# One expert input block beside each group of routing weights, one-hot tiles built a group ahead, and weights read back by eight expert blocks

## The chip, the cores and the metric

The kernel runs on one core of one Trainium2 chip. The metric is the device time of one execution in microseconds (us). Several executions are timed and their median is given. One more execution is recorded with the hardware profiler.

## What is computed

One layer of a backbone for 512 latent tokens (768 with the context) of width 1024: a mixer (state-space scan, pooling, neighbourhood attention), an output projection, and then a product-key expert network, the PEER part. The change touches the last part alone:

```python
def peer_ffn(u, w_q, sub_keys, u_tab, v_tab):
    q = (t @ w_q).reshape(n_tok, 8, 2, 128)
    s = einsum('thid,hikd->thik', q, sub_keys)
    v1, i1 = top_k(s[:, :, 0], 16); v2, i2 = top_k(s[:, :, 1], 16)
    ...
    idx = take_along_axis(cand_idx, pos)          # 128 experts of 16384 for each token
    g = softmax(top_s)
    act = gelu(einsum('tkd,td->tk', u_tab[idx], x))
    return einsum('tk,tkd->td', g * act, v_tab[idx])
```

So each of 512 tokens picks 8 x 16 = 128 experts out of 16384. An expert has an input row (in `peer_u`) and an output row (in `peer_v`), both of width 1024.

## The kernel before

The expert tables are cut into 128 blocks of 128 experts. For 384 of the 512 tokens (three tiles of 128) the kernel works densely: for every block `a` it multiplies the tokens with all 128 input rows (here an **input block** or U block: `u_block`, 24 matmuls of 384 columns, since every product is made of three float32r products of a high and a low part), applies gelu, multiplies with a 128 x 384 tile of routing weights that is zero wherever a token did not choose an expert, and multiplies the result with the 128 output rows (a **value block** or V block: `e_v`, 18 matmuls of 512 columns, summed in PSUM over all 128 blocks). The last 128 tokens are worked by gathering: for each of 128 **slots** `k`, GpSimd (POOL) gathers one expert row (input and output row side by side) for each of the 128 tokens (`g_load`), VectorE (DVE) makes the dot product with the token (`g_dot`), ScalarE (ACT) its gelu and its weight (`g_act`), and DVE adds the weighted output row to a sum (`g_acc`). The rows sit in four buffers.

An input block needs nothing of the routing, so 74 of the 128 (`NAHEAD`, the list `AHEAD`) are made ahead of the expert loop: `ahead_steps` is a generator, and each `next(ahead)` makes one of them. In a step it first takes the low parts left from the step before (DVE), then fetches coming blocks, splits the block two steps on into its high part (ACT, line 177) and leaves the low part (DVE, line 180) to the next step, then runs the 24 matmuls, the gelu (ACT) and writes the result to DRAM (`act_d`, issued by ACT).

The **routing weights stage** (`weights_T`, lines 1559 to 1594) turns expert numbers and softmax weights into dense weight tiles. 384 tokens are taken in 48 groups of eight (three calls of 16). For each group DVE builds one-hot tiles from the numbers: `oi` (line 1567, 16 bit, 2048 elements for each partition) and `ow`, the one-hot times the weight's high and low part (line 1571, two instructions). TensorE (PE) multiplies them, 16 matmuls of 128 columns for each group (lines 1578 and 1579, into `gdps`), ACT copies the results into a staging tile (`stg`, line 1581, two for each group), and after each fourth group 2 MB are written to DRAM (`gd_d`). Beside it run input blocks (`next(ahead)` where `q8 in UQ`: three of four groups) and slots of the gathered tokens (one for four groups, so 12 here). All is issued under `manual_schedule`: each engine takes its instructions in the order in which the code is written.

The **expert loop** (lines 1759 to 1794) goes over all blocks. At step `i` SyncE (SP) issues reads for blocks ahead: the stored result of an input block made ahead (`acl`, at `i+6`) or the input rows (`wraw<-in_peer_ut`, at `i+6`), the output rows (`wraw<-in_peer_uv`, at `i+4`) and, for every fourth block, the routing weights of four blocks (`e_weights`, 768 KB in runs of 512 bytes, at `i+5`). DVE and ACT multiply by the weights and split for block `i+1`, PE runs the input block `i+2` if it was not made ahead (54 are left), and then value block `i`. The gathers' slots 12 to 127 are spread evenly over the first 121 steps (`kG`). SP takes its reads in order, and a read waits at the head of the queue until its buffer is free or its source is written.

Of the kernel before, what the change touches and what calls it, by code (L numbers as in the profile page):

```python
# [7 lines left out]
F32 = mybir.dt.float32  # L8
# [138 lines left out]
NAHEAD = 74  # L147
# [3 lines left out]
def build(tc, A, out, dbg=None):  # L151
# [1405 lines left out]
    gq = {}  # L1557

    def weights_T(t):
        for q8 in range(16):  # L1560
            if q8 % 4 == 0:
                stg = sg.tile([P, P, TQ], F32, name="stg")

            def tb(ap):
                return ap[:, t * 16 + q8].rearrange("p w (g c) -> p (w g) c", c=2).unsqueeze(2).broadcast_to([P, 8, P, 2])
            oi = gs2.tile([P, 2, 4, P, 2], F16, name="oi", bufs=3)
            V.tensor_tensor(oi.rearrange("p w g b c -> p (w g) b c"), iotaA.unsqueeze(1).broadcast_to([P, 8, P, 2]), tb(ixT), ALU.is_equal)
            ob, oa = oi[:, 0], oi[:, 1]
            ow = gs2.tile([P, 2, 4, P, 2], F16, name="ow", bufs=3)
            for w in range(2):  # L1570
                V.tensor_tensor(ow[:, w], oa, tb(gwT)[:, w * 4:w * 4 + 4], ALU.mult)
            oh, ol = ow[:, 0], ow[:, 1]
            for q4 in range(2):
                ps = psD.tile([P, 4, P], F32, name="gdps")
                for j in range(4):
                    tt = q4 * 4 + j
                    pr, c = tt // 2, tt % 2
                    PE.matmul(ps[:, j, :], ob[:, pr, :, c], oh[:, pr, :, c], start=True, stop=False)
                    PE.matmul(ps[:, j, :], ob[:, pr, :, c], ol[:, pr, :, c], start=False, stop=True)  # L1579
                t0 = q8 % 4 * 8 + q4 * 4  # L1580
                S.activation(stg[:, :, t0:t0 + 4].rearrange("p a t -> p t a"), ps, AF.Copy, scale=1.0 / GSCALE)  # L1581
            if q8 % 4 == 3:
                (nc.gpsimd if t == 2 and q8 == 15 else nc.scalar).dma_start(gd_d[t * 4 + q8 // 4], stg)
            if q8 in UQ:
                next(ahead, None)
            k = t * 4 + q8 // 4
            gq[0] = stg
            if q8 % 4 == 0:
                if k:
                    g_acc(k - 1)  # L1590
                    g_load(k + 3)
                g_dot(k)
            elif q8 % 4 == 1:
                g_act(k)

    UQ = (0, 1, 3, 4, 5, 7, 8, 9, 11, 12, 13, 15)
# [21 lines left out]
    go_ahead(2)  # L1618
# [8 lines left out]
    for t in range(3):  # L1627
        weights_T(t)
    g_acc(11)
    g_load(15)  # L1630
# [10 lines left out]
    gl = glp.sb("gl", bufs=3)  # L1641
# [24 lines left out]
    def e_weights(a):  # L1666

        if a % 4 == 0:
            n = NQ if a else NQ - 1
            gd = gds[a // 4] = gls[a // 4 % 2].tile([P, NQ, 4 * TQ], F32, name="gd", bufs=1)  # L1670
            nc.sync.dma_start(gd[:, 0:n, :], gd_d[0:n, :, a:a + 4, :].rearrange("q b a t -> b q (a t)"))
            if n < NQ:
                G.tensor_copy(gd[:, n, :], gq[0][:, 0:4, :].rearrange("p a t -> p (a t)"))

# [7 lines left out]
    def e_w(a):  # L1682

        x = ac.pop(a)
        xq = x.rearrange("p (q t) -> p q t", q=NQ)
        V.tensor_tensor(xq, xq, gds[a // 4][:, :, a % 4 * TQ:(a % 4 + 1) * TQ], ALU.mult)  # L1686
# [13 lines left out]
    def f_load():  # L1700

        nc.sync.dma_start(fgr, A["rowg"][:, D:2 * D])
        for t in (3, 0, 1, 2):
            nc.sync.dma_start(hx[:, t, :], h_d[t * P:(t + 1) * P, :])
        row_bc(g2r, psu, 2, 2)

    def f_mul(t, hf):

        if hf == 0:
            sqs[t] = gt.tile([P, 2 * D], F32, name="row")  # L1710
            fss[t] = e1.tile([P, 2], F32, name="fss", bufs=2)
        sq = sqs[t]
        hs = slice(hf * 512, (hf + 1) * 512)
        src = accT[t][hf] if t < 3 else accG[:, hs]
        if "peer" in dbg:
            V.tensor_copy(sq[:, hs], src)
            nc.sync.dma_start(dbg["peer"][t * P:(t + 1) * P, hs], sq[:, hs])
        V.tensor_tensor(sq[:, hs], src, g2r[:, hs], ALU.mult)
        (V if t == 2 else G).tensor_tensor(hx[:, t, hs], sq[:, hs], hx[:, t, hs], ALU.add)

    def f_sq(t, hf):
        hs = slice(hf * 512, (hf + 1) * 512)
        S.activation(sqs[t][:, hs], hx[:, t, hs], AF.Square, accum_out=fss[t][:, hf:hf + 1])
# [5 lines left out]
    def f_gain(t, hf):  # L1729
        hs = slice(hf * 512, (hf + 1) * 512)  # L1730
        (V if t == 2 else G).tensor_tensor(sqs[t][:, D + hf * 512:D + hf * 512 + 512], hx[:, t, hs], fgr[:, hs], ALU.mult)
# [18 lines left out]
    kG = [12 + min(P - 12, (i * (P - 12) + 120) // 121) for i in range(P + 1)]  # L1750
    with order:
# [6 lines left out]
        hx = e1.tile([P, NX, D], F32, name="hx")  # L1758
        for i in range(-6, P + 1):
            within(lambda a: e_load(a, 0), i + 6)  # L1760
            within(lambda a: e_load(a, 1), i + 4)
            if i > -5:
                within(e_weights, i + 5)
# [19 lines left out]
            if i == 64:  # L1783
                f_load()
            if i == P - 4:
# [58 lines left out]
```

## Time and profile before

| what | before |
| --- | --- |
| median of 3 runs | 1888.75 us |
| lowest and highest | 1887.59 and 1889.18 us |
| the profiled execution's own time | 1889.47 us |
| its span in the profile | 1887.6 us |
| PE busy, DVE busy, ACT busy, POOL busy | 96%, 72%, 45%, 18% |
| DMA, mean over the span | 237 GB/s |

The profile gives for every instruction its start and duration, and for idle time of an engine what ended it. A matmul's duration is modelled and overlaps the next one, so the spacing of starts, not the busy share, tells how fast PE goes. The routing weights stage lasts from about 887 to 1101 us, the expert loop from there to the end. A read or write through DMA is given by the time from its issue to its landing.

### The profile page before, as it was taken

What the parts mean: (1) busy time and instruction counts of PE and PEld (TensorE: products, weight loads), DVE (VectorE), ACT (ScalarE), POOL (GpSimd) and SP (SyncE); (2) the same over time, 40 slices, a digit from 0 to 9 for tenths busy, and PEclk for the clock granted to TensorE, in tenths of its full rate; (3) what the DMA queues carried; (4) which work ended last, traced back from release to release, by engine and by line L of the source; (5) the groups of instructions that cost most, each with busy time, mean ns of one, the idle gap of its engine ahead of it and who ended that gap; (6) DMA issues with size and microseconds to landing.
All of it is one profiled execution on the core that took longest, in us unless ns stands there. A gap on an engine that the chain in (4) does not pass through costs nothing.

```text
span 1887.6 us, 26321 instructions
## 1 busy us (share of the span) xinstructions
PE 1805.8 (96%) x9703; PEld 1521.7 (81%) x9703; DVE 1363.1 (72%) x2681; ACT 845.7 (45%) x1552; POOL 348.4 (18%) x261
## 2 busy tenths in 40 slices
PE   7999999986899999999999999999999999999997
PEld 4677776654677888999988898888888888888886
DVE  5553137797653459987788878887888887888875
ACT  4332226534653433345767654443443443443444
POOL 1101300151012544420011011111111111111103
PEclk9999999997999999999999999999999999999999
DMA  9546332217423533474787889999999999999971
GB/s 364 165 140 200 85 123 67 68 53 229 149 74 100 163 111 111 135 253 156 266 301 287 289 317 387 351 332 357 356 328 353 373 351 351 370 325 345 366 256 62
DMA packets 210193, 446.74 MB, mean 237 GB/s; under 512 B 13424, under 2 KB 137072, under 8 KB 192112
## 3 DMA queue, kind: packets, MB, share of 16 engines
q1 hardware_dynamic: 172192, 259.25, 41.1%
q0 software_dynamic: 18576, 136.32, 18.7%
q10 hardware_dynamic: 19296, 49.49, 7.2%
q8 instruction: 76, 1.25, 0.3%
q14 instruction: 53, 0.43, 0.1%
HBM read 394.81 MB, written 52.30 MB: 237 GB/s over the span
## 4 chain that ended last, share of the span: by engine, by line
PE 82%; DVE 7%; ACT 6%; issue 2%; DMA 1%; POOL 0%; ACTq 0%; DVEq 0%; SPq 0%; POOLq 0%
PE pv L188 9%; PE pv L187 9%; PE pv L189 9%; PE pu L187 8%; PE pu L189 8%; PE pu L188 8%; PE acc L187 5%; PE acc L189 5%; PE acc L188 5%; ACT stg L1581 2%; PE acc L419 2%; PE acc L421 2%; PE acc L423 1%; DVE wl L180 1%; ACT wh L177 1%
## 5 line engine op out<-in xcount | busy, mean ns | idle before, releaser
L180 DVE TENSOR_TENSOR wl<-wraw,wh 128x1024 fp32r<-128x1024 f32 x290 | 355.2, 1241 | 190.9 <-ACT wh L177 182.3
L177 ACT ACTIVATE wh<-wraw 128x1024 fp32r<-128x1024 f32 x324 | 336.1, 1053 | 223.8 <-PE acc L188 76.8
L187 PE MATMUL pu<-u2h,wh 128*128 128x384 f32 (+2 forms) x1040 | 354.8, 341 | 0.0
L189 PE MATMUL pu<-u2h,wl 128*128 128x384 f32 (+2 forms) x1040 | 350.4, 337 | 1.5 <-DVE wl L180 1.5
L188 PE MATMUL pu<-u2l,wh 128*128 128x384 f32 (+2 forms) x1040 | 350.3, 337 | 0.0
L188 PE MATMUL pv<-wl,wwh 128*128 128x512 f32 x768 | 303.2, 395 | 0.0
L187 PE MATMUL pv<-wh,wwh 128*128 128x512 f32 x768 | 303.1, 395 | 0.0
L189 PE MATMUL pv<-wh,wwl 128*128 128x512 f32 x768 | 303.1, 395 | 0.0
L1524 POOL DMA_INDIRECT row<-in_peer_uv,idxG x128 | 138.7, 1084 | 844.4 <-DVE accG L1538 746.0
L187 PEld LDWEIGHTS pu<-u2h,wh 128*128 128x128 f32 x1040 | 196.6, 189 | 3.1 <-ACT g2r L1092 0.7
L188 PEld LDWEIGHTS pu<-u2l,wh 128*128 128x128 f32 x1040 | 196.6, 189 | 2.3
L189 PEld LDWEIGHTS pu<-u2h,wl 128*128 128x128 f32 x1040 | 196.3, 189 | 1.9 <-DVE wl L180 1.8
L189 PEld LDWEIGHTS pv<-wh,wwl 128*128 128x128 f32 x768 | 144.4, 188 | 34.4
L188 PEld LDWEIGHTS pv<-wl,wwh 128*128 128x128 f32 x768 | 144.4, 188 | 32.1 <-DVE wl L180 0.2
L187 PEld LDWEIGHTS pv<-wh,wwh 128*128 128x128 f32 x768 | 144.3, 188 | 32.0
L1538 DVE SCALAR_TENSOR_TENSOR accG<-row,wG,accG 128x1024 f32<-128x1024 f32 x127 | 162.5, 1279 | 0.0
L1529 DVE CUSTOM_DVE_ANT_0 row<-row,u2G 128x1024 f32<-128x1024 f32 x128 | 156.2, 1220 | 0.0
L1686 DVE TENSOR_TENSOR act<-act,gd 128x384 f32<-128x384 f32 x54 | 31.3, 579 | 131.3 <-ACT act L1680 131.3
L177 ACT ACTIVATE wwh<-acl 128x384 fp32r<-128x384 f32 x74 | 38.9, 526 | 191.4 <-DVE acl L1686 157.8
L1680 ACT ACTIVATE act<-pu 128x384 f32<-128x384 f32 x54 | 26.6, 492 | 207.3 <-PE pu L189 207.3
L1581 ACT ACTIVATE stg<-gdps 128x512 f32<-128x512 f32 x96 | 98.0, 1161 | 26.7 <-PE gdps L1579 21.9
L180 POOL TENSOR_TENSOR wl<-wraw,wh 128x1024 fp32r<-128x1024 f32 x34 | 81.7, 2403 | 112.5 <-ACT wh L177 94.0
(403 smaller groups left out, 3111.7 us busy)
## 6 DMA issues: line engine op xcount, KB each, us to landing
wraw<-in_peer_ut SPq DMA_DIRECT2D x128, 512.0 KB, 5.4
wraw<-in_peer_uv SPq DMA_DIRECT2D x128, 512.0 KB, 9.5
gd<-gd_d SPq DMA_DIRECT2D x31, 768.0 KB, 12.7
gd_d<-stg ACTq DMA_DIRECT2D x11, 2048.0 KB, 6.7
wraw<-in_w_in SPq DMA_DIRECT2D x36, 512.0 KB, 4.1
acl<-act_d SPq DMA_DIRECT2D x74, 192.0 KB, 6.6
act_d<-act ACTq DMA_DIRECT2D x72, 192.0 KB, 5.0
kT<-in_ada_w SPq DMA_DIRECT2D x18, 512.0 KB, 4.8
```

The source lines that it names most:

```text
L177: S.activation(hi, full, AF.Copy)
L180: (eng or V).tensor_tensor(lo, full, hi.bitcast(F32), ALU.subtract)
L187: PE.matmul(ps, ah, bh, start=start, stop=False)
L188: PE.matmul(ps, ah, bl, start=False, stop=False)
L189: PE.matmul(ps, al, bh, start=False, stop=stop)
L419: PE.matmul(px, h[:, k, :], uh[:, k, :], start=s, stop=False)
L421: PE.matmul(px, h[:, k, :], ul[:, k, :], start=False, stop=False)
L1524: G.indirect_dma_start(out=rows[k], out_offset=None, in_=A["peer_uv"], in_offset=bass.IndirectOffsetOnAxis(ap=idxG[:, k:k + 1], axis=0))
L1529: V.tensor_tensor_reduce(row[:, 0:D], row[:, 0:D], u2G, 1.0, 0.0, ALU.mult, ALU.add, actG[:, k:k + 1])
L1538: V.scalar_tensor_tensor(accG, row[:, D:2 * D], wG[:, k:k + 1], accG, ALU.mult, ALU.add)
L1581: S.activation(stg[:, :, t0:t0 + 4].rearrange("p a t -> p t a"), ps, AF.Copy, scale=1.0 / GSCALE)
L1686: V.tensor_tensor(xq, xq, gds[a // 4][:, :, a % 4 * TQ:(a % 4 + 1) * TQ], ALU.mult)
```

## The change

- `NAHEAD` goes from 74 to 86, so 12 more input blocks are made ahead and 42 instead of 54 are left for the expert loop.
- The routing weights stage is written as 48 equal groups `n`, with one input block beside every group (48 instead of 36). One input block that stood ahead of the stage's last preparation now stands between the first one-hot tiles and the first group.
- The one-hot tiles are built by `hot(n + 1)` at the start of group `n`, one group ahead of their matmuls.
- 24 slots of the gathered tokens instead of 12 are taken in this stage, one for two groups (`NMID`).
- In the loop the remaining 104 slots are spread by the number of blocks that PE runs (`done`: a step with an input block counts double), not by steps.
- The routing weights are read by eight blocks (1.5 MB in runs of 1024 bytes) into two buffers, with four blocks at either end, and one step earlier. The pool of `acl` tiles grows from 3 to 4 buffers.
- The residual rows `hx`, needed at the very end, are read at step 122 instead of 64, into a weights buffer and the tile `u2G` that are free by then.

```diff
-NAHEAD = 74
+NAHEAD = 86
...
+    NMID = 24
+    hots = {}
+    def hot(n):
+        def tb(ap):
+            return ap[:, n].rearrange("p w (g c) -> p (w g) c", c=2).unsqueeze(2).broadcast_to([P, 8, P, 2])
+        oi = gs2.tile([P, 2, 4, P, 2], F16, name="oi", bufs=3)
+        V.tensor_tensor(oi.rearrange("p w g b c -> p (w g) b c"), iotaA.unsqueeze(1).broadcast_to([P, 8, P, 2]), tb(ixT), ALU.is_equal)
+        ow = gs2.tile([P, 2, 4, P, 2], F16, name="ow", bufs=3)
+        for w in range(2):
+            V.tensor_tensor(ow[:, w], oi[:, 1], tb(gwT)[:, w * 4:w * 4 + 4], ALU.mult)
+        hots[n] = (oi[:, 0], ow[:, 0], ow[:, 1])
+    def weights_T(n):
+        if n % 4 == 0:
+            gq[0] = sg.tile([P, P, TQ], F32, name="stg")
+        stg = gq[0]
+        if n + 1 < TD // 8:
+            hot(n + 1)
+        ob, oh, ol = hots.pop(n)
+        for q4 in range(2):
...
+            S.activation(stg[:, :, t0:t0 + 4].rearrange("p a t -> p t a"), ps, AF.Copy, scale=1.0 / GSCALE)
+        if n % 4 == 3:
+            (nc.gpsimd if n == TD // 8 - 1 else nc.scalar).dma_start(gd_d[n // 4], stg)
+        k = n // 2
+        if n % 2:
+            g_act(k)
+        next(ahead, None)
+        if n % 2 == 0:
+            if k:
+                g_acc(k - 1)
+                g_load(k + 3)
+            g_dot(k)
...
-    go_ahead(2)
+    go_ahead(1)
     slots_T(2)
...
-    for t in range(3):
-        weights_T(t)
-    g_acc(11)
-    g_load(15)
+    hot(0)
+    go_ahead(1)
+    for n in range(TD // 8):
+        weights_T(n)
+    g_acc(NMID - 1)
+    g_load(NMID + 3)
...
-        if a % 4 == 0:
+        if a % 8 == 4 or a == 0:
+            m = 8 if 0 < a < P - 4 else 4
...
+                gd = gls[1].tile([P, NQ, 8 * TQ], F32, name="gd", bufs=2)
+            nc.sync.dma_start(gd[:, 0:n, :], gd_d[0:n, :, a:a + m, :].rearrange("q b a t -> b q (a t)"))
...
+    def h_load():
+        hr = gls[1].tile([P, NQ, 8 * TQ], F32, name="gd", bufs=2).rearrange("p q t -> p (q t)")
         for t in (3, 0, 1, 2):
+            hx[t] = u2G if t == 3 else hr[:, t * D:(t + 1) * D]
+            nc.sync.dma_start(hx[t], h_d[t * P:(t + 1) * P, :])
...
-    kG = [12 + min(P - 12, (i * (P - 12) + 120) // 121) for i in range(P + 1)]
+    done = [sum(1 if a + 2 in AHEAD else 2 for a in range(i)) for i in range(P + 1)]
+    kG = [NMID + min(P - NMID, -(-done[i] * (P - NMID) // done[P - 8])) for i in range(P + 1)]
...
-                within(e_weights, i + 5)
+                within(e_weights, i + 6)
...
+            if i == P - 6:
+                h_load()
```

The first place is DVE in the routing weights stage. Before, from one slot's dot product (`L1529`) on, four groups with three low parts of input blocks (`L180`, `wl`) between them:

```order
L1529 ISA row,actG<-row,u2G 128x1024
L1529 ISA actG 128x1
L1567 TENSOR_TENSOR oi<-iotaA,ixT 128x2048
L1571 TENSOR_TENSOR ow<-oi,gwT 128x1024 x2
L180 TENSOR_TENSOR wl<-wraw,wh 128x1024
L1567 TENSOR_TENSOR oi<-iotaA,ixT 128x2048
L1571 TENSOR_TENSOR ow<-oi,gwT 128x1024 x2
L1567 TENSOR_TENSOR oi<-iotaA,ixT 128x2048
L1571 TENSOR_TENSOR ow<-oi,gwT 128x1024 x2
L180 TENSOR_TENSOR wl<-wraw,wh 128x1024
L1567 TENSOR_TENSOR oi<-iotaA,ixT 128x2048
L1571 TENSOR_TENSOR ow<-oi,gwT 128x1024 x2
```

Now, from a slot's dot product to the next slot's sum (`L1538`), the same engine and stage:

```order
L1529 ISA row,actG<-row,u2G 128x1024
L1529 ISA actG 128x1
L1567 TENSOR_TENSOR oi<-iotaA,ixT 128x2048
L1570 TENSOR_TENSOR ow<-oi,gwT 128x1024 x2
L180 TENSOR_TENSOR wl<-wraw,wh 128x1024
L1567 TENSOR_TENSOR oi<-iotaA,ixT 128x2048
L1570 TENSOR_TENSOR ow<-oi,gwT 128x1024 x2
L180 TENSOR_TENSOR wl<-wraw,wh 128x1024
L1538 SCALAR_TENSOR_TENSOR accG<-row,wG,accG 128x1024
```

Every group has a low part now, and a slot comes after two groups instead of four. The one-hot tiles of a row pair are those of the group after.

The second place is SP's queue where the expert loop begins (`gd` are routing weights, `acl` stored input results, `ut` input rows, `uv` output rows). Before:

```order
L1671 DMA gd<-gd_d 128x11x128
L1650 DMA acl<-act_d 128x384 x3
L208 DMA wraw<-in_peer_uv 128x1024
L208 DMA wraw<-in_peer_ut 128x1024
L208 DMA wraw<-in_peer_uv 128x1024
L1671 DMA gd<-gd_d 128x12x128
L1650 DMA acl<-act_d 128x384
L208 DMA wraw<-in_peer_uv 128x1024
```

Now:

```order
L1680 DMA gd_11053<-gd_d 128x11x128
L1655 DMA acl<-act_d 128x384 x3
L208 DMA wraw<-in_peer_ut 128x1024
L208 DMA wraw<-in_peer_uv 128x1024
L1680 DMA gd<-gd_d 128x12x256
L1655 DMA acl<-act_d 128x384
L208 DMA wraw<-in_peer_uv 128x1024
```

The second read of weights is twice as large, and the output rows of block 3 (the second `uv` here) now stand behind it, where before they stood ahead of it. That read needs the last 2 MB of weights in DRAM.

## Rows read from the trace of the kernel before

**Rows 1.** Stretches (us): busy us (instructions) by engine, clock granted to PE, DMA share, GB/s.

```profile
887.00:1101.00 214.00, 199.21 (x1608) 190.44 (x1608) 182.85 (x213) 147.37 (x187) 18.40 (x11) 0.99 0.76 275
...
1114.00:1830.00 716.00, 716.00 (x3372) 618.70 (x3371) 588.89 (x759) 296.24 (x577) 109.82 (x112) 1.00 0.95 349
```

**Rows 2.** Who waited for whom, 890 to 1106 us: total us, times, longest.

```profile
DVE wl L180 <- ACT wh L177: 32.7, 12, 4.3
...
PEld L1578 <- DVE ow L1571: 13.8, 11, 1.3
```

**Rows 3.** Timeline of PE before the first group: start us, us [idle before <- releaser].

```profile
883.33 0.27 PE L1547 MATMUL pt<-cst,g 128*128 128x128 f32 x1
887.05 0.22 PE L1578 MATMUL gdps<-ow,oi 128*128 128x128 f16 x1 [3.45 <-DVE ow L1571]
```

**Rows 4.** The stretch of the first group (columns as rows 1).

```profile
887.00:890.00 3.00, 2.57 (x19) 2.44 (x19) 3.00 (x5) 1.41 (x2) 0.00 (x0) 0.56 0.17 11
```

**Rows 5.** Timeline of PE: first matmul of an input block, of two groups, of a block.

```profile
985.57 0.42 PE L187 MATMUL pu<-u2h,wh 128*128 128x384 f32 x1
...
989.88 0.24 PE L1578 MATMUL gdps<-ow,oi 128*128 128x128 f16 x1
...
991.70 0.42 PE L187 MATMUL pu<-u2h,wh 128*128 128x384 f32 x1
```

**Rows 6.** Who waited for whom, 1114 to 1830 us: the longest wait of PE.

```profile
PEld pu L187 <- ACT g2r L1092: 0.7, 1, 0.7
```

**Rows 7.** Groups of instructions, 1200 to 1700 us, value and input blocks.

```profile
L189 PE MATMUL pv<-wh,wwl 128*128 128x512 f32 x502 | 198.1, 395 | 0.0
...
L187 PE MATMUL pu<-u2h,wh 128*128 128x384 f32 x281 | 95.1, 339 | 0.0
```

**Rows 8.** Timeline of DVE in the routing weights stage.

```profile
996.88 1.23 DVE L180 TENSOR_TENSOR wl<-wraw,wh 128x1024 fp32r<-128x1024 f32 x1 [2.53 <-ACT wh L177]
998.02 1.28 DVE L1538 SCALAR_TENSOR_TENSOR accG<-row,wG,accG 128x1024 f32<-128x1024 f32 x1
999.22 1.22 DVE L1529 CUSTOM_DVE_ANT_0 row<-row,u2G 128x1024 f32<-128x1024 f32 x1
...
1000.36 1.22 DVE L1567 TENSOR_TENSOR oi<-iotaA,ixT 128x2048 f16<-128x2048 f16 x1
1001.61 1.29 DVE L1571 TENSOR_TENSOR ow<-oi,gwT 128x1024 f16<-128x1024 f16 x2
1002.82 1.22 DVE L180 TENSOR_TENSOR wl<-wraw,wh 128x1024 fp32r<-128x1024 f32 x1
```

**Rows 9.** Timeline of ACT in the same stretch.

```profile
990.97 0.20 ACT L1532 ACTIVATE actG<-actG 128x1 f32<-128x1 f32 x1 [0.40 <-DVE ow L1571]
...
991.41 3.97 ACT L1581 ACTIVATE stg<-gdps 128x512 f32<-128x512 f32 x4
...
996.75 0.47 ACT L1302 ACTIVATE act<-pu 128x384 f32<-128x384 f32 x1
...
999.51 1.08 ACT L177 ACTIVATE wh<-wraw 128x1024 fp32r<-128x1024 f32 x1
```

**Rows 10.** Line 1524, gathers, 890 to 1106 us: ns min/median/max.

```profile
L1524 POOL DMA_INDIRECT row<-in_peer_uv,idxG x12: 1670/1672/1788, 908.5 to 1105.9; - x12
```

**Rows 11.** Line 1524, 1200 to 1700 us.

```profile
L1524 POOL DMA_INDIRECT row<-in_peer_uv,idxG x80: 936/1008/1015, 1200.2 to 1697.7; - x80
```

**Rows 12.** Line 1567, one-hot tiles, whole span.

```profile
L1567 DVE TENSOR_TENSOR oi<-iotaA,ixT x48: 1217/1220/1225, 885.1 to 1097.5; 128x2048 f16<-128x2048 f16 x48
```

**Rows 13.** DMA of the loop, 1114 to 1830 us.

```profile
DMA packets 98756, 249.76 MB, mean 349 GB/s; under 512 B 6274, under 2 KB 61696, under 8 KB 84203
```

**Rows 14.** Tile wraw, loop: issue to landing (min/median/max) of input and output rows.

```profile
DMA to landing us min/median/max: 6.2/9.9/18.2
```

**Rows 15.** The write of line 1583: issue to landing, eleven by ACT, one by POOL.

```profile
L1583 POOL DMA_DIRECT2D gd_d<-stg x1: 579/579/579, 1105.0 to 1105.0; - x1
...
DMA to landing us min/median/max: 6.3/6.7/13.3
```

More of the change, by code (lines that the diff above doesn't have):

```diff
@@ L1557, in build @@
     gq = {}
[L1559 to L1594, printed above, removed]
@@ new lines, in weights_T @@
+    def weights_T(n):
[6 more added lines that the diff above has]
+        for q4 in range(2):
+            ps = psD.tile([P, 4, P], F32, name="gdps")
+            for j in range(4):
+                pr, c = q4 * 2 + j // 2, j % 2
+                PE.matmul(ps[:, j, :], ob[:, pr, :, c], oh[:, pr, :, c], start=True, stop=False)
+                PE.matmul(ps[:, j, :], ob[:, pr, :, c], ol[:, pr, :, c], start=False, stop=True)
+            t0 = n % 4 * 8 + q4 * 4
+            S.activation(stg[:, :, t0:t0 + 4].rearrange("p a t -> p t a"), ps, AF.Copy, scale=1.0 / GSCALE)
[10 more added lines that the diff above has]
+            g_dot(k)
@@ L1640, in build @@
     glp = Pools()
-    gl = glp.sb("gl", bufs=3)
+    gl = glp.sb("gl", bufs=4)
     gls = [gl]
@@ L1666, in e_weights @@
     def e_weights(a):
-        if a % 4 == 0:
+        if a % 8 == 4 or a == 0:
+            m = 8 if 0 < a < P - 4 else 4
             n = NQ if a else NQ - 1
-            gd = gds[a // 4] = gls[a // 4 % 2].tile([P, NQ, 4 * TQ], F32, name="gd", bufs=1)
-            nc.sync.dma_start(gd[:, 0:n, :], gd_d[0:n, :, a:a + 4, :].rearrange("q b a t -> b q (a t)"))
+            if m == 4:
+                gd = gls[0].tile([P, NQ, 4 * TQ], F32, name="gd4", bufs=1)
+            else:
+                gd = gls[1].tile([P, NQ, 8 * TQ], F32, name="gd", bufs=2)
+            nc.sync.dma_start(gd[:, 0:n, :], gd_d[0:n, :, a:a + m, :].rearrange("q b a t -> b q (a t)"))
             if n < NQ:
                 G.tensor_copy(gd[:, n, :], gq[0][:, 0:4, :].rearrange("p a t -> p (a t)"))
+            for j in range(m):
+                gds[a + j] = gd[:, :, j * TQ:(j + 1) * TQ]
     def e_u(a):
@@ L1702, in f_load @@
         nc.sync.dma_start(fgr, A["rowg"][:, D:2 * D])
+        row_bc(g2r, psu, 2, 2)
+    hx = {}
+    def h_load():
+        hr = gls[1].tile([P, NQ, 8 * TQ], F32, name="gd", bufs=2).rearrange("p q t -> p (q t)")
         for t in (3, 0, 1, 2):
-            nc.sync.dma_start(hx[:, t, :], h_d[t * P:(t + 1) * P, :])
-        row_bc(g2r, psu, 2, 2)
+            hx[t] = u2G if t == 3 else hr[:, t * D:(t + 1) * D]
+            nc.sync.dma_start(hx[t], h_d[t * P:(t + 1) * P, :])
     def f_mul(t, hf):
@@ L1718, in f_mul @@
         V.tensor_tensor(sq[:, hs], src, g2r[:, hs], ALU.mult)
-        (V if t == 2 else G).tensor_tensor(hx[:, t, hs], sq[:, hs], hx[:, t, hs], ALU.add)
+        (V if t == 2 else G).tensor_tensor(hx[t][:, hs], sq[:, hs], hx[t][:, hs], ALU.add)
     def f_sq(t, hf):
         hs = slice(hf * 512, (hf + 1) * 512)
-        S.activation(sqs[t][:, hs], hx[:, t, hs], AF.Square, accum_out=fss[t][:, hf:hf + 1])
+        S.activation(sqs[t][:, hs], hx[t][:, hs], AF.Square, accum_out=fss[t][:, hf:hf + 1])
     def f_rstd(t):
@@ L1730, in f_gain @@
         hs = slice(hf * 512, (hf + 1) * 512)
-        (V if t == 2 else G).tensor_tensor(sqs[t][:, D + hf * 512:D + hf * 512 + 512], hx[:, t, hs], fgr[:, hs], ALU.mult)
+        (V if t == 2 else G).tensor_tensor(sqs[t][:, D + hf * 512:D + hf * 512 + 512], hx[t][:, hs], fgr[:, hs], ALU.mult)
     def f_norm(t):
@@ L1757, in build @@
         fgr = e1.tile([P, D], F32, name="fgr")
-        hx = e1.tile([P, NX, D], F32, name="hx")
         for i in range(-6, P + 1):
```

3 lines of the change are left out of this document (1 added, 2 removed).

## The prediction

> **What bounds the kernel now.** I read the stretches first [rows 1]. In the expert loop PE is busy for all of 716 us, at a granted clock of 1.00, that is 2.4 GHz, and the longest wait charged to it is 0.7 us [rows 6]. So the loop's length is the number of PE blocks times their pace, and everything else there is hidden. In the routing weights stage PE is busy for 199 of 214 us only. The waits of that stretch say why [rows 2]: DVE stands still for 32.7 us, twelve times, for a high part that ACT has not made yet, and PE stands for 13.8 us, eleven times, for one-hot tiles that DVE then makes late. Twelve is the number of rounds of four groups. One of the four has no input block, its tiles are built in the place where they are needed, and the engines wait round in a circle: ACT copies four results in a row, is late with the high part, DVE with its low part, the slot and the next tiles, and PE gets those late. So the two stages have different limits, and PE work moved from the loop into this stage first fills idle time.
>
> **The idle time, measured.** An input block takes 4.31 us from its first matmul to the next group, and two groups take 1.82 us, so 0.91 us each [rows 5]. Between the end of the transposes at 883.60 [rows 3] and the start of the input block that follows the last group, at 1101.0, where I cut the stretch [rows 1], there are 217.4 us with 48 groups and 35 input blocks (the order of PE's instructions gives that count). Their work is 48 x 0.91 + 35 x 4.31 = 43.7 + 150.9 = 194.6 us. **22.8 us are idle or slow.** Some 5 us of it lie at the front: 3.45 us of waiting for the first tiles [rows 3], and then a first group whose clock was granted at 0.56 on the mean, so mostly the lower level of 1.2 GHz, after that gap [rows 4].
>
> **The loop's pace.** From 1200 to 1700 us there are three rows of 502, 501 and 501 matmuls of value blocks (the first stands in [rows 7]), 83.6 blocks of 18, and three of 281 of input blocks, 35.1 of 24. That is 118.7 blocks in 500 us: 4.21 us each, for either kind.
>
> **The change part by part.**
>
> *Twelve input blocks leave the loop:* -12 x 4.21 = -50.5 us, all on the path, since PE has no gap there.
>
> *The stage gets them.* It has one more input block than the 12: one that stood ahead of the transposes now follows the first tiles, which only moves the stage's start forward by 4.31. If PE never waits, the stage takes 48 x (0.91 + 4.31) = 250.6 us from a start 4.31 us earlier, against 217.4: +28.9 us. Whether PE never waits is the question, so I add up the other engines for a pair of groups, in which PE needs 2 x 5.22 = 10.44 us. DVE, from start to start: low part 1.14, sum 1.20, dot product 1.14, `oi` 1.25, both `ow` 1.21 [rows 8]; a pair has two low parts and tiles and one slot, 2 x 3.60 + 2.34 = 9.54 us. ACT goes from a gelu through two copies to the end of a split in 3.84 us (996.75 to 1000.59), and a slot's two small ones take 0.44 [rows 9]; 2 x 3.84 + 0.44 = 8.1 us, and the issue of a write each fourth group does not change that. Both fit, DVE with 0.90 us to spare in a pair.
>
> They must also fit in order. DVE now builds tiles a group before PE wants them, so a late tile has 5.2 us before it hurts. A low part is taken one step after its high part and one step before its matmuls. ACT ends a split some 4 to 4.5 us after a group begins, the low part is due in the group after that, DVE comes to it after 2.5 us of tiles, and the slot stands behind it. I find no place where the circle closes. A slot's row is gathered three pairs, 31 us, before its dot product.
>
> *Transfers of the stage.* 48 x (0.52 MB input rows + 0.20 MB results + 0.52 MB weights) + 24 x 1.05 MB of gathers = 85 MB in 250.6 us, 339 GB/s. Now 275 GB/s take 0.76 of the DMA engines' time [rows 1], which makes 362 at full. It fits, with little to spare; input rows are read several blocks ahead.
>
> *Twelve more slots here, twelve fewer in the loop.* The gathers' issue takes 1.67 us on POOL here [rows 10] against 1.01 in the loop [rows 11]; POOL has nothing else to do, so I take nothing. What speaks against more gathers here is that they might hold DVE instead. But all 48 `oi` took 1.217 to 1.225 us [rows 12], with gathers beside some of them. So far it is POOL that is held up. The Trainium skill (SBUF — State Buffer, "Who interferes with whom") says that VectorE and GpSimd share one pair of ports, and that of two instructions that want it the second one to issue is fully blocked. By that rule a gather that issues first would cost DVE its own length, and the stage would be DVE's; by the row it costs nothing, and I go by the row. The other way is rival C.
>
> *The loop's slots by PE blocks; weights by eight blocks; `acl` by four buffers.* The loop's bytes fall from 249.8 MB [rows 13] by twelve input blocks (6.3) and twelve slots (12.6) and rise by twelve stored results (2.4), to 233 MB in 665.5 us: 350 GB/s, as now. DVE loses 12 x (2.34 + 1.14) = 42 of 589 us of work, in step with the time. So neither comes nearer to being a bound. A read of 1.5 MB takes 2.25 us more than one of 768 KB at 349 GB/s, and output rows queue behind it. They land after 9.9 us in the middle and 18.2 at worst [rows 14] and are issued about three steps, 12.6 us at least, before their split, and PE never waited for the worst. Cost over the loop between 0 and 34 us (15 reads); nearest are the rows without a wait; I take 1 us.
>
> *Start of the loop.* The second read of weights must wait for the last write, issued 4 us after the last group and landing in 13.3 at most [rows 15]; the output rows of block 3 are now behind it. PE has seven blocks, 29.6 us, before it needs them: 17.3 us of write, a read of 9.9 to 18.2 us, 2.3 us of split make 29.5 to 37.8. Cost 0 to 8 us; I take 1, near the middle landing.
>
> *`hx` read late.* Its buffers are free by step 120; one read stands behind it. 2.1 MB take 6 us, with no gathers left; 0 to 3 us, I take 0.
>
> **Sum.** -50.5 + 28.9 + 1 + 1 = -19.6 us. The profiled execution took 1889.5 us (span 1887.6 and 1.9 around it), which gives 1869.9; the median of the runs lies 0.7 us below it, so **1869.2 us**.
>
> **The rivals.**
>
> A. *DVE's wait for the high part comes back.* Before, it is 2.53 us where shown [rows 8], once a round. For: DVE is 91% full in the new stage. Against: the round with four copies in a row, which made ACT late, is gone. Once in four groups, it adds (9.54 + 1.27 - 10.44) x 24 = 9 us: **1878 us**.
>
> A2, the other side: *the wait falls in every pair.* Then (9.54 + 2.53 - 10.44) x 24 = 39 us are lost in the stage: **1908 us**, slower. It decides from 0.90 + 19.6 / 24 = 1.7 us of waiting in a pair on.
>
> B. *Output rows come late behind each large read*, and PE waits 2.25 us for each of 15: **1903 us**. From 1.3 us for each on, the change loses. Against: PE's missing waits in the loop.
>
> C. *Gathers hold DVE*, 1.67 us in each pair: (11.21 - 10.44) x 24 = 18.5 us: **1888 us**. Against: [rows 12].
>
> D. *The change does not do what it says:* the tiles ahead sit in DVE's queue behind a low part that waits, come no earlier, and the idle time stays. Then only the 1.2 us between 4.31 and 4.21 move: **1890 us**. Against: the order puts them ahead of the low part.
>
> **How the numbers follow.** Forecast 0.78, A 0.08, A2 0.03, B 0.04, C 0.03, D 0.02; the rest, 0.02, for a gain beyond the idle time, which nothing shows. A measurement of this kernel can tell about 0.2%, 3.8 us, from no change. Faster: 0.78 + 0.08 + 0.02 = 0.88. Same: C and D, 0.05. Slower: A2 and B, 0.07. The lower end is the idle time with no cost at all and some scatter, 1866; the upper takes in A and the larger half of the start's cost, 1879. That leaves out some 0.14.
>
> **What would show it.** Right: a stage of about 250 us with groups 5.2 us apart and hardly an idle PE, no gap and no low clock before its first group, and a loop some 50 us shorter without waits of PE. Wrong: DVE waiting for ACT's high parts inside the stage with PE behind it (A), `oi` or `ow` longer than 1.3 us beside a gather (C), PE waiting for low parts of output rows once in eight blocks (B), or a gap at block 3 or 4.

## The result, and the profile after the change

The changed kernel takes **1869.24 us** (median of 5 runs, 1868.25 to 1877.89), the kernel before 1888.75 us (5 runs). The ratio is 0.9913, 95% interval 0.9899 to 0.9927: faster by about 0.9%. The forecast was 1869.2 us with a range from 1866 to 1879. The profiled execution took 1869.24 us with a span of 1867.1 us, against 1889.47 and 1887.6 before: **20.5 us** less span.

The page of the kernel after, its busy shares and the first line of its chain:

```profile
PE 1796.6 (96%) x9703; PEld 1515.9 (81%) x9703; DVE 1371.2 (73%) x2681; ACT 850.3 (46%) x1552; POOL 366.6 (20%) x261
...
PE 87%; DVE 4%; ACT 4%; DMA 2%; issue 2%; POOL 0%; SPq 0%; ACTq 0%; DVEq 0%; POOLq 0%
```

The shares say almost nothing: PE was at 96% before and is at 96% now. The stretches say more (columns as in [rows 1]; the routing weights stage, then the expert loop; the first two lines are the stage's front, which [rows 4] showed before):

```profile
877.00:881.00 4.00, 4.00 (x25) 4.00 (x24) 2.52 (x4) 1.96 (x5) 0.00 (x0) 1.00 0.43 167
881.00:884.00 3.00, 3.00 (x29) 2.83 (x28) 2.97 (x4) 2.08 (x3) 0.00 (x0) 1.00 0.37 105
884.00:1127.00 243.00, 243.00 (x1869) 235.53 (x1868) 223.51 (x259) 172.38 (x233) 38.57 (x23) 1.00 0.91 327
1143.00:1808.00 665.00, 664.24 (x3077) 567.13 (x3076) 549.23 (x709) 274.80 (x526) 112.40 (x100) 1.00 0.94 348
```

In the stage PE is now busy for all of 243 us, at a granted clock of 1.00, while DMA works at a share of 0.91 and DVE for 223.5 of the 243 us. The front, where PE stood for 3.45 us and then ran its first group at 0.56 [rows 3, 4], has a clock of 1.00 and no gap. The groups follow each other at an even pace, as PE's timeline shows (first matmul of a group, first one of its input block):

```profile
985.53 0.24 PE L1585 MATMUL gdps<-ow,oi 128*128 128x128 f16 x1
986.43 0.42 PE L187 MATMUL pu<-u2h,wh 128*128 128x384 f32 x1
...
990.74 0.24 PE L1585 MATMUL gdps<-ow,oi 128*128 128x128 f16 x1
991.64 0.42 PE L187 MATMUL pu<-u2h,wh 128*128 128x384 f32 x1
```

That is 5.21 us for a group with its block. DVE needs 9.59 us for a pair of groups, from one slot's sum to the next (its timeline), where PE needs 10.42:

```profile
986.84 1.28 DVE L1538 SCALAR_TENSOR_TENSOR accG<-row,wG,accG 128x1024 f32<-128x1024 f32 x1
...
995.28 1.23 DVE L180 TENSOR_TENSOR wl<-wraw,wh 128x1024 fp32r<-128x1024 f32 x1
996.43 1.28 DVE L1538 SCALAR_TENSOR_TENSOR accG<-row,wG,accG 128x1024 f32<-128x1024 f32 x1
```

The waits of 884 to 1127 us, beside [rows 2] (us in total, times, longest). DVE still waits for ACT's high parts, for half as long and never over 1.7 us, and PE has no wait for a tile left:

```profile
DVE wl L180 <- ACT wh L177: 17.3, 21, 1.7
```

For what follows I cut each trace in the same way: the **stage** runs from the end of the transposes to the start of the input block that follows the last group, the **loop** from there to PE's last matmul.

| us | before | after | difference |
| --- | --- | --- | --- |
| end of the transposes | 883.6 | 877.2 | -6.4 |
| stage | 217.5 | 250.1 | +32.6 |
| loop | 774.8 | 727.7 | -47.1 |
| rest | 11.8 | 12.2 | +0.4 |
| span | 1887.6 | 1867.1 | -20.5 |

Of the -6.4, 4.31 are the input block that moved behind the transposes. The other 2.1 lie in a part of the program that the change does not touch, and there two executions of the changed kernel differ by 2.3 (877.2 and 879.5, the last section). So stage and loop together, counted from the same input block on, fell from 996.5 (992.2 + 4.3) to 977.7 us: **18.8 us** are the change.

### The profile page after: what moved, and what is told of

Read it like the earlier page. It is cut to its first block, busy times and chain, and to the rows that moved or that the text cites. A ratio compares the mean times of both kernels' runs of the same rounds, so it can differ in the third digit from the quotient of the medians.

```text
span 1867.1 us, 26410 instructions
## 1 busy us (share of the span) xinstructions
PE 1796.6 (96%) x9703; PEld 1515.9 (81%) x9703; DVE 1371.2 (73%) x2681; ACT 850.3 (46%) x1552; POOL 366.6 (20%) x261
## 4 chain that ended last, share of the span: by engine, by line
PE 87%; DVE 4%; ACT 4%; DMA 2%; issue 2%; POOL 0%; SPq 0%; ACTq 0%; DVEq 0%; POOLq 0%
PE pu L187 10%; PE pu L189 10%; PE pu L188 10%; PE pv L188 9%; PE pv L189 9%; PE pv L187 9%; PE acc L187 5%; PE acc L188 5%; PE acc L189 5%; PE acc L419 2%; PE acc L421 2%; PE acc L423 1%; PE gdps L1585 1%; PE gdps L1586 1%; PE mm L844 1%
## 5 line engine op out<-in xcount | busy, mean ns | idle before, releaser
L180 DVE TENSOR_TENSOR wl<-wraw,wh 128x1024 fp32r<-128x1024 f32 x290 | 357.3, 1244 | 189.7 <-ACT wh L177 187.8
L177 ACT ACTIVATE wh<-wraw 128x1024 fp32r<-128x1024 f32 x324 | 337.0, 1052 | 223.5 <-PE acc L188 76.1
L1524 POOL DMA_INDIRECT row<-in_peer_uv,idxG x128 | 157.2, 1228 | 814.2 <-DVE accG L1538 719.8
L1538 DVE SCALAR_TENSOR_TENSOR accG<-row,wG,accG 128x1024 f32<-128x1024 f32 x127 | 162.5, 1279 | 4.7 <-ACT wG L1533 3.4
L1529 DVE CUSTOM_DVE_ANT_0 row<-row,u2G 128x1024 f32<-128x1024 f32 x128 | 155.1, 1219 | 0.0
L177 ACT ACTIVATE wwh<-acl 128x384 fp32r<-128x384 f32 x86 | 45.2, 526 | 204.3 <-DVE acl L1697 138.9
L180 POOL TENSOR_TENSOR wl<-wraw,wh 128x1024 fp32r<-128x1024 f32 x34 | 81.7, 2404 | 113.6 <-ACT wh L177 95.2
L1691 ACT ACTIVATE act<-pu 128x384 f32<-128x384 f32 x42 | 20.6, 490 | 162.9 <-PE pu L189 162.9
L1697 DVE TENSOR_TENSOR act<-act,gd 128x384 f32<-128x384 f32 x42 | 23.4, 558 | 90.2 <-ACT act L1691 90.1
```

The costliest lines, as they stand in the source:

```text
L177: S.activation(hi, full, AF.Copy)
L180: (eng or V).tensor_tensor(lo, full, hi.bitcast(F32), ALU.subtract)
L1524: G.indirect_dma_start(out=rows[k], out_offset=None, in_=A["peer_uv"], in_offset=bass.IndirectOffsetOnAxis(ap=idxG[:, k:k + 1], axis=0))
L1529: V.tensor_tensor_reduce(row[:, 0:D], row[:, 0:D], u2G, 1.0, 0.0, ALU.mult, ALU.add, actG[:, k:k + 1])
L1538: V.scalar_tensor_tensor(accG, row[:, D:2 * D], wG[:, k:k + 1], accG, ALU.mult, ALU.add)
L1697: V.tensor_tensor(xq, xq, gds.pop(a), ALU.mult)
```

## The experiments

The question was which part earns the 18.8 us, and where the loop lost 3.4 us of the 50.5 that twelve blocks at 4.21 us should have freed. My theory was the forecast's: the moved blocks fill the idle time, with the tiles ahead as their condition. The rivals were that the tiles ahead earn all of it without any block moved, that the blocks do it without the tiles, and that each block moved earns a little (18.8 / 12 = 1.6 us). Every table below gives stage, loop, their sum, the gain of the sum against the 996.5 of before, and the ratio of times with its 95% interval. Edits are against the changed kernel unless it says otherwise.

### The tiles ahead without the blocks

Two kernels do this one thing from either side. The first is the changed kernel with 74 blocks ahead and 12 slots in the stage, so of the change the front, the tiles a group ahead, the read-back, the loop's spacing of slots, four `acl` buffers and the late read of `hx` are left:

```diff
-NAHEAD = 86
+NAHEAD = 74
...
-    NMID = 24
+    NMID = 12
...
-        k = n // 2
-        if n % 2:
+        k = n // 4
+        if n % 4 == 1:
             g_act(k)
-        next(ahead, None)
-        if n % 2 == 0:
+        if n % 4 != 2:
+            next(ahead, None)
+        if n % 4 == 0:
```

> The changed kernel with 74 blocks made ahead, an input block beside three of four groups and 12 slots in the stage, as before the change; the tiles are still built a group ahead, and reads by eight blocks, slots by PE blocks and the late residual rows stay. Theory (the gain is idle time, which either half of the change removes): the stage falls from 217 to 199 to 205 us, the loop keeps its length, the time is 1869 to 1876 us. Rival (the blocks moved out of the loop bring the gain, 1.6 us each): no more than 4 us below the kernel before, 1885 us or more.

The second is the kernel *before* with the tiles ahead and the block at the front, and nothing else: its weights read by four, its slots by steps, `hx` read early, three `acl` buffers. (`hot` has the lines that it has in the change.)

```diff
...
+            if t * 16 + q8 < 47:
+                hot(*divmod(t * 16 + q8 + 1, 16))
+            ob, oh, ol = hots.pop(t * 16 + q8)
...
-    go_ahead(2)
+    go_ahead(1)
     slots_T(2)
...
+    hot(0, 0)
+    go_ahead(1)
     for t in range(3):
         weights_T(t)
```

> The kernel before with one part of the change alone: tiles built a group ahead, the first ones ahead of the input block that precedes the first group. 74 blocks, 12 slots, reads by four blocks, slots by steps and the early residual rows stay as before. Theory (all of the gain is the stage's idle time, and the tiles ahead alone remove it; all other parts of the change are worth nothing or cost a little): stage 199 us, loop 774.8 us as before, the time 1863.5 to 1867 us, below the changed kernel. Rival (reads by eight blocks, slots by PE blocks or four acl buffers have a share): 1870 us or more.

| kernel | stage | loop | sum | gain | median | ratio |
| --- | --- | --- | --- | --- | --- | --- |
| after | 250.1 | 727.7 | 977.7 | 18.8 | 1869.24 | 0.9913 (0.9899 to 0.9927) |
| tiles ahead, 74 blocks | 198.9 | 774.8 | 973.6 | 22.9 | 1865.21 | 0.9882 (0.9867 to 0.9897) |
| before + tiles ahead | 198.9 | 774.7 | 973.6 | 22.9 | 1866.25 | 0.9879 (0.9863 to 0.9896) |

Both say the same. By the forecast's own terms a stage without idle time is 48 x 0.91 + 36 x 4.31 = 198.8 us, and that is what both show. The tiles ahead and the front alone give back the 22.8 us that were idle or slow. In each round of four groups the one without a block is still there, and DVE's waits for high parts fell all the same, from the 32.7 us of [rows 2] to these (884 to 1076 us; first kernel, second kernel):

```profile
DVE wl L180 <- ACT wh L177: 8.7, 10, 1.1
```

```profile
DVE wl L180 <- ACT wh L177: 9.2, 10, 1.9
```

The only wait of a matmul in the second kernel, from 880 to 1870 us, is

```profile
PE gdps L1586 <- DVE ow L1569: 0.4, 1, 0.4
```

and in the first one PE is busy at a clock of 1.00 throughout (stage, loop):

```profile
884.00:1075.00 191.00, 190.64 (x1567) 184.95 (x1566) 180.69 (x212) 146.42 (x185) 18.45 (x11) 1.00 0.86 310
1090.00:1830.00 740.00, 740.00 (x3481) 638.94 (x3481) 605.07 (x776) 307.87 (x589) 126.27 (x112) 1.00 0.93 342
```

The twelve blocks that move make the stage 51.2 us longer (250.06 - 198.85) and the loop 47.1 us shorter (774.76 - 727.65). They **cost 4.1 us**, and 5.5 by the second execution of the changed kernel further down, whose loop is 1.4 us longer. The slots, which differ too, have no share (the section on slots). Since the first kernel's loop is as long as the loop before (774.8), reading by eight blocks, the slots by PE blocks, four `acl` buffers and the late read of `hx` cost nothing and earn nothing there; the rest behind the loop is 0.4 us longer with them (12.2 for 11.8). The first kernel's time, 1865.21 us, lies below the 1869 to 1876 that I expected: I had taken the blocks for a part of the gain.

### The blocks without the tiles ahead

```diff
-        if n + 1 < TD // 8:
-            hot(n + 1)
+        if n:
+            hot(n)
```

> The changed kernel with one edit: the one-hot tiles of group n are built at the start of group n, not a group ahead; the input block beside every group stays. Theory (the gain is the stage's idle time, and one block beside each group lets VectorE run ahead by itself, since it needs 9.5 us of a pair's 10.4): tiles come 0 to 0.5 us late in every second group, the stage is 250 to 262 us, the time 1869 to 1881 us, most of the gain kept. Rival (the lookahead of the tiles is what removes the idle time): PE waits for tiles in most groups, 0.4 us or more each, the stage is 265 us or more and the time 1884 us or more.

| kernel | stage | loop | sum | gain | median | ratio |
| --- | --- | --- | --- | --- | --- | --- |
| tiles in place | 258.1 | 726.9 | 985.0 | 11.5 | 1878.5 | 0.995 (0.9936 to 0.9963) |

This kernel keeps the front, since its first tiles still stand ahead of a block. Of the 18.0 us that the rounds of four groups lost (next experiment), 8.1 are left, so the block beside every group takes away more than half by itself. The group without a block, behind which ACT copied four results in a row, is gone; that this is the reason fits, but is not shown: DVE's waits for high parts in the stage are 26.1 us in 23 times (32.7 in 12 before), only none is longer than 2.3 us (4.3 before). What stays of PE's waits is a short one in each round; the waits from 875 to 1870 us:

```profile
PE gdps L1586 <- DVE ow L1570: 4.4, 12, 0.4
...
PEld L1585 <- DVE ow L1570: 3.8, 11, 0.4
```

4.4 + 3.8 = 8.2 us, and the stage is 8.1 us longer than after (258.13 - 250.06). So with the blocks in place the tiles ahead are worth 8 us; without the blocks they are worth 18.0 (22.9 above, less the 4.9 of the front in the next experiment).

### The front alone

The kernel *before*, with one input block between the first tiles and the first group, its tiles otherwise in place:

```diff
-    go_ahead(2)
+    go_ahead(1)
     slots_T(2)
...
+            if t == 0 and q8 == 0:
+                go_ahead(1)
```

> The kernel before with one edit: one input block that stood ahead of the last transposes now stands between the first group's tiles and its matmuls. All later tiles are built in place as before. Theory (of the 22.8 us idle, some 5 lie at the front: 3.5 us of gap and a first group at the low clock): no gap and a granted clock of 1.00 at the first group, 4.5 to 5.5 us faster than the kernel before, the rounds of 18.2 us stay. Rival (the front's gap is made up elsewhere in the stage, since ACT and VectorE set the rounds' pace anyway): less than 2 us.

| kernel | stage | loop | sum | gain | median | ratio |
| --- | --- | --- | --- | --- | --- | --- |
| front only | 216.8 | 774.8 | 991.6 | 4.9 | 1884.33 (11 runs) | 0.9975 (0.9966 to 0.9984) |

4.9 us, where the forecast had "some 5 us" at the front. The clock of the stage's first 12 us is 1.00:

```profile
878.00:890.00 12.00, 11.62 (x88) 11.17 (x87) 10.63 (x13) 7.20 (x12) 0.00 (x0) 1.00 0.49 171
```

and the rounds of four groups stay what they were, with the waits of [rows 2]:

```profile
PEld L1580 <- DVE ow L1571: 14.1, 12, 1.3
```

So the 22.9 us are 4.9 of the front and 18.0 of the rounds.

### Four blocks more

```diff
-NAHEAD = 86
+NAHEAD = 90
...
         next(ahead, None)
+        if n % 12 == 5:
+            next(ahead, None)
```

> The changed kernel with 90 blocks made ahead instead of 86: four groups of the stage have two input blocks beside them. Theory (the stage has no idle time left, so a block moved there earns nothing): stage 17 us longer, loop 17 us shorter, the time within 2 us of the changed kernel. Rival (each block moved out of the loop earns what the change showed for each, 19.5 / 12 = 1.6 us): 6.5 us faster than the changed kernel.

| kernel | stage | loop | sum | gain | median | ratio |
| --- | --- | --- | --- | --- | --- | --- |
| 90 blocks ahead | 266.7 | 709.8 | 976.5 | 20.1 | 1870.45 | 0.9906 (0.9891 to 0.9921) |

The stage grows by 16.6 us and the loop shrinks by 17.9, 4 x 4.16 and 4 x 4.47. The sum is 1.2 us lower, the time is not; at the loop's start PE has no wait in this execution, and such waits differ from one execution to the next (the section on the start of the loop). PE work that is moved costs on the new side about what it saved on the old one; the 1.6 us for each block of the rival would have been 6.5.

### Slots

Twelve slots instead of 24 in the stage (so 116 in the loop); and, in another kernel, 24 slots there but the loop's slots spread by steps, as before:

```diff
-    NMID = 24
+    NMID = 12
...
-        k = n // 2
-        if n % 2:
+        k = n // 4
+        if n % 4 == 1:
             g_act(k)
         next(ahead, None)
-        if n % 2 == 0:
+        if n % 4 == 0:
```

> The changed kernel with 12 slots of the gathered tokens in the stage instead of 24, one for four groups; the other 116 in the loop. Theory (PE bounds both stages, VectorE has room in both): no difference from the changed kernel beyond 2 us, stage 250 us. Rival (VectorE is near enough to its limit in the stage that slots cost there): 3 us or more faster than the changed kernel. Other rival (the loop is near VectorE's or the transfers' limit): 3 us or more slower.

```diff
-    kG = [NMID + min(P - NMID, -(-done[i] * (P - NMID) // done[P - 8])) for i in range(P + 1)]
+    kG = [NMID + min(P - NMID, (i * (P - NMID) + 119) // 120) for i in range(P + 1)]
```

> The changed kernel with the 104 slots left to the loop spread by steps, as before, not by PE blocks. Theory (VectorE is 82% full in the loop and has room in either spacing): loop 727 to 728.5 us, no difference. Rival (in short steps without an input block VectorE is then over its time, and PE waits for low parts): loop 730 us or more.

| kernel | stage | loop | sum | gain | median | ratio |
| --- | --- | --- | --- | --- | --- | --- |
| 12 slots | 250.0 | 727.7 | 977.7 | 18.8 | 1868.45 | 0.9899 (0.9884 to 0.9915) |
| slots by steps | 250.0 | 727.4 | 977.4 | 19.1 | 1870.16 | 0.9905 (0.9890 to 0.9920) |

Neither part of the change shows a worth: 0.0 and 0.3 us are less than what loops of the same code differ by (see the start of the loop). With 116 slots the loop moves 367 GB/s in place of 348, at a DMA share of 0.97, and PE is busy for the same 664.24 of 665 us:

```profile
1143.00:1808.00 665.00, 664.24 (x3078) 567.16 (x3077) 575.13 (x746) 281.20 (x551) 126.78 (x112) 1.00 0.97 367
```

### The end of the loop

In the kernel after, PE has four waits behind the stage, 2.4 us in all (1127 to 1867 us):

```profile
PE pv L188 <- DVE wl L180: 2.1, 3, 0.8
PE pv L187 <- ACT wh L177: 0.3, 1, 0.3
```

Three of them are in the last blocks. There VectorE's instructions become slow, as its timeline shows:

```profile
1818.79 0.55 DVE L1697 TENSOR_TENSOR acl<-acl,gd 128x384 f32<-128x384 f32 x1
...
1836.77 1.65 DVE L1697 TENSOR_TENSOR acl<-acl,gd 128x384 f32<-128x384 f32 x1
...
1840.01 2.23 DVE L180 TENSOR_TENSOR wl<-wraw,wh 128x1024 fp32r<-128x1024 f32 x1
1842.16 1.64 DVE L1697 TENSOR_TENSOR acl<-acl,gd 128x384 f32<-128x384 f32 x1
```

In the same microseconds GpSimd works on the gathered tokens' last rows: it adds the residual rows and multiplies by the gains, part of the final steps (its timeline):

```profile
1836.33 3.24 POOL L1737 TENSOR_TENSOR u2G<-row,u2G 128x512 f32<-128x512 f32 x2 [54.46 <-DVE row L1736]
1839.54 3.84 POOL L1749 TENSOR_TENSOR row<-u2G,fgr 128x512 f32<-128x512 f32 x2
```

The Trainium skill ("SBUF — State Buffer", section "Who interferes with whom") says that a VectorE instruction with two inputs in SBUF contends with a GpSimd instruction that reads SBUF. Here the trace agrees: 0.55 becomes 1.65 us, and a low part of 1.23 us takes 2.23.

The same work slowed VectorE before as well (the kernel before, where the operation has line 1686):

```profile
1859.79 1.68 DVE L1686 TENSOR_TENSOR act<-act,gd 128x384 f32<-128x384 f32 x1 [3.65 <-ACT act L1680]
```

but there it stood beside an input block. With 86 blocks ahead the last one left in the loop is 125 and runs at step 123; with 74 it was 126, at step 124, where this work is. In the next kernel the work comes two steps earlier, where block 125 covers it, and the row it needs is read earlier:

```diff
-        for t in (3, 0, 1, 2):
-            hx[t] = u2G if t == 3 else hr[:, t * D:(t + 1) * D]
+        for t in range(3):
+            hx[t] = hr[:, t * D:(t + 1) * D]
             nc.sync.dma_start(hx[t], h_d[t * P:(t + 1) * P, :])
...
+            if i == P - 8:
+                hx[3] = u2G
+                nc.sync.dma_start(u2G, h_d[3 * P:4 * P, :])
...
-            if i == P - 4:
+            if i == P - 6:
                 f_mul(3, 0)
                 f_mul(3, 1)
-            if i == P - 3:
+            if i == P - 5:
```

> The changed kernel with the work on the gathered tokens' last rows moved two steps earlier (the read of their residual rows to step 120, the product to step 122, squares and gains to step 123, under the last input block). Theory (the last input block lies one step before that work now, and VectorE's instructions, stretched beside GpSimd's, are exposed at the end): PE's waits in the last three blocks go, loop 2 to 2.6 us shorter, 725 to 725.7 us. Rival (the waits come from the late read of residual rows): they stay or grow.

| kernel | stage | loop | sum | gain | median | ratio |
| --- | --- | --- | --- | --- | --- | --- |
| end two steps earlier | 250.0 | 725.1 | 975.2 | 21.4 | 1867.57 | 0.9884 (0.9867 to 0.9900) |

2.5 us of the loop are back. The late read of `hx` is not the cause: with 74 blocks ahead, in the first experiment, the read is as late and no wait stands there. One wait of PE is left from 880 to 1870 us:

```profile
PE pv L188 <- DVE wl L180: 0.7, 1, 0.7
```

### The start of the loop

That last wait stands 31 us into the loop. In the kernel after, on PE:

```profile
1158.02 0.50 PE L188 MATMUL pv<-wl,wwh 128*128 128x512 f32 x1 [0.77 <-DVE wl L180]
```

and the high part that it goes back to waited for output rows (ACT):

```profile
1155.65 1.06 ACT L177 ACTIVATE wh<-wraw 128x1024 fp32r<-128x1024 f32 x1 [3.54 <-DMA wraw<-in_peer_uv]
```

On SP's queue the read of those rows was issued 2.5 us behind the second read of weights, which stood there for the last write (`L1680` is the read of weights; both `L208` are reads of output rows):

```profile
1130.53 0.38 SPq L208 DMA_DIRECT2D wraw<-in_peer_uv  x1
...
1141.25 0.38 SPq L1680 DMA_DIRECT2D gd<-gd_d  x1
...
1143.78 0.80 SPq L208 DMA_DIRECT2D wraw<-in_peer_uv  x1
```

The forecast had this order as the cause. The first kernel here is that of the section above, with block 3's rows moved ahead of that read:

```diff
-                within(e_weights, i + 6)
+                if i != -2:
+                    within(e_weights, i + 6)
+                if i == -1:
+                    e_weights(4)
```

> As the run with the tail, and the second read of weights placed behind the output rows of block 3 at the loop's start. Theory (block 3's rows queue behind that read, which waits for the last write): the wait of PE some 25 us into the loop goes too, loop 724 to 724.5 us, the time 3 to 4 us below the changed kernel. Rival (the large read itself takes the bandwidth there): the wait stays.

The other one leaves the order and halves the size: the changed kernel with all weights read by four blocks, into the same buffers.

```diff
-        if a % 8 == 4 or a == 0:
-            m = 8 if 0 < a < P - 4 else 4
+        if a % 4 == 0:
+            m = 4
```

> The changed kernel with the routing weights read by four blocks as before (768 KB, 512-byte runs), at the new place in the queue. Theory (at the loop's start PE is some 1 us late because the first rows land behind a write and a read of 1.5 MB): with half the read the wait some 30 us into the loop goes, loop 726.5 us; the rest of the loop is the same, since PE bounds it. Rival (the wait for the last write alone sets it): the wait stays and the loop is 727.7 us. Other rival (larger runs ease the transfers): PE waits elsewhere in the loop, 729 us or more.

| kernel | stage | loop | sum | gain | median | ratio |
| --- | --- | --- | --- | --- | --- | --- |
| end earlier, rows of block 3 first | 250.0 | 724.8 | 974.8 | 21.7 | 1866.87 | 0.9882 (0.9866 to 0.9899) |
| reads by four | 250.1 | 726.1 | 976.2 | 20.4 | 1868.39 | 0.9887 (0.9872 to 0.9903) |

With the rows of block 3 first, that block's split waits for nothing any more. PE's wait stands a block later, and the high part that it goes back to is that of block 4, whose rows now stand behind the read (PE, then ACT):

```profile
1161.06 0.50 PE L188 MATMUL pv<-wl,wwh 128*128 128x512 f32 x1 [0.66 <-DVE wl L180]
```

```profile
1158.68 1.06 ACT L177 ACTIVATE wh<-wraw 128x1024 fp32r<-128x1024 f32 x1 [3.04 <-DMA wraw<-in_peer_uv]
```

So the order decides which block is late, as the forecast had it: the one whose rows are issued right behind the read. That the loop gains only 0.3 us is no proof against it, since the delay is passed on. The size counts too: with the smaller read in the old place neither of the two splits waits, PE's waits at the start are gone (of its list three remain, 1.6 us in all, in the last blocks) and the loop is 1.5 us shorter. With 74 blocks ahead the same large read causes no wait (the first experiment); PE runs five input blocks there before value block 3, here four. What the wait for the last write adds, no run separates.

The size of this loss is known only roughly. The loop of the kernel with its tiles in place is the changed kernel's, and so is that of the next section: they took 726.9, 727.7 and 729.1 us, and they part in the first 41 us, where block 3's split waited 3.01, 3.54 and 4.89 us for its rows and PE's matmuls have waits of 0, 0.77 and 1.98 us there. The 0.3 and the 1.5 us above, each from one execution, are to be read beside that.

### The changed kernel again

> The changed kernel again, on the same chip as the runs beside it, so that these can be compared. Theory: 1868 to 1872 us, loop 727.7 us (3.4 below what twelve blocks of 4.21 would leave), waits of PE for low parts at the loop's start and in the last three blocks.

Run beside the kernel before with tiles ahead, on the same chip: stage 250.0, loop 729.1, sum 979.1 us, median 1869.9, ratio 0.9895 (0.9879 to 0.9912). Two waits at the loop's start were 1.21 and 0.77 us here. The intervals of the two kernels' ratios overlap; the cut of the traces, 979.1 against 973.6, is plain.

**The best version** of those run is thus not the whole change but its smallest part: the tiles a group ahead and a block at the front, with 74 blocks ahead, 1865 to 1866 us.

## Why the prediction was right, and where it was not

**The idle time** (22.8 us): right. The kernels with the tiles ahead and the front alone gain 22.9, the front 4.9 of it.

**What the stage would take:** 250.6 forecast, 250.06 measured, with DVE's pair at 9.59 us for 9.54 and PE's at 10.42 for 10.44. The engines' sums for a pair of groups decided it.

**The loop:** -50.5 forecast, -47.1 measured. The pace held within what can be told here. Two terms of the sum were mis-sized. *Start of the loop*, taken as 1 within 0 to 8, measured about 1.5 (0.8 and 3.0 in two other executions, against the loop with the smaller read), and its mechanism, rows of block 3 behind the second read, held; the size of that read, which I had costed apart, has its share in it. *`hx` read late*, taken as 0 within 0 to 3: the end of the loop lost 2.5 us, and not through the read. I costed the transfer and never asked which input block had covered the work at step 124. The list of blocks made ahead changes with their number, and so does the last block left. The two come to 4.0 us where the loop fell short by 3.4; the 0.6 between them I cannot place.

**Large reads** (1 us taken, 0 to 34): away from the loop's start nothing.

**What the gain comes from:** here the forecast's reading failed, though its sum held. "PE work moved from the loop into this stage first fills idle time" makes the moved blocks the earner. In the sum -50.5 + 28.9 the gain looks like their move. The runs show in its place that the tiles ahead and the block at the front take all of the idle time without a block moved (22.9 us), and that the move on top costs 4.1 us: the twelve blocks take 51.2 us in the stage, where the forecast has 50.5 for them in the loop (0.7), and the loop falls 3.4 short of that.

**The total.** In the profiled execution the span fell by 20.5 us where 19.6 were forecast: 0.6 less in the stage, 1.4 more in the loop (3.4 lost for 2), 0.4 more in the rest, and 2.1 less ahead of the stage, which is not the change's. Without that last the step would have been 18.4 us. That the median lies within 0.1 us of the forecast is luck: the terms missed in both directions, and the 2.1 us are not the change's.

**The rivals.** A and A2: DVE's waits for high parts are there, 17.3 us in 21 of them, but at most 1.7 us long, and none reaches PE. B: PE has no wait that goes back to output rows but at the loop's start. D: the tiles do come earlier. C: the gathers do not hold DVE. All 48 `oi` took 1.215 to 1.225 us with twice as many gathers (one gather ran from 988.39 for 1.68 us, an `oi` from 989.18 for 1.22), while the gathers' issue took 1.67 us on POOL as before:

```profile
L1567 DVE TENSOR_TENSOR oi<-iotaA,ixT x48: 1215/1220/1225, 878.7 to 1117.6; 128x2048 f16<-128x2048 f16 x48
```

```profile
L1524 POOL DMA_INDIRECT row<-in_peer_uv,idxG x23: 1672/1677/1681, 895.2 to 1123.1; - x23
```

The rule that I weighed there (the Trainium skill, "SBUF — State Buffer", "Who interferes with whom", the second to issue is fully blocked) thus does not bind `oi` beside a gather's issue in this kernel. I had applied it too widely: the sentence of that section cited for the loop's end speaks, for a VectorE instruction with two inputs, of GpSimd instructions that read SBUF, and beside such ones, GpSimd's additions and multiplications at the loop's end, VectorE does slow down. Whether a gather's issue is one, no run shows.

## What to carry to other kernels

When idle time is due to work that is made too late, make it earlier, and measure that alone before moving other work on top: here the lookahead and the block at the front earned 22.9 us, and the twelve blocks moved with them gave 4.1 back. When the number of pieces made ahead changes, look at what the last piece left had been covering, and at what the first ones now have to cover. Add up each engine for one period of a stage: those sums forecast the stage to 0.6 us in 250.

## What was not expected of the hardware

The stage repeats to 0.1 us between kernels with the same code (seven stages between 249.99 and 250.06 us), and so do the four loops after 74 blocks (774.7 to 774.8). The loops after 86 blocks do not, for the waits at their start, and still less does the point where the stage begins: 875.2 to 883.1 us with the same instructions ahead of it. Much of it arises between 400 and 500 us, where PE is busy for 71 to 76 us of 100 and its granted clock differs from execution to execution. Before, after, and after again:

```profile
400.00:500.00 100.00, 74.73 (x410) 50.98 (x410) 75.97 (x212) 45.11 (x122) 18.98 (x14) 0.86 0.56 178
```

```profile
400.00:500.00 100.00, 71.36 (x425) 48.86 (x425) 78.98 (x221) 46.84 (x124) 19.31 (x14) 0.95 0.59 184
```

```profile
400.00:500.00 100.00, 75.72 (x410) 51.26 (x410) 75.99 (x213) 45.30 (x122) 19.63 (x14) 0.86 0.58 178
```

With 0.95 the stretch holds 425 matmuls, with 0.86 it holds 410. The last two are the same kernel, and their stages begin at 877.2 and 879.5 us. So effects of a few us are to be read from a stretch of the trace, not from the span of one execution; what makes the clock differ was not tried.
